# Wider weight splits, wider expert chunks and a convolution that reads its PSUM bank, in a two-layer diffusion trunk on one core

## Chip, cores and metric

One NeuronCore of a Trainium2 chip runs the whole program. The time is device microseconds of one execution, from launch to end. Its engines are TensorE (PE: matmuls; PEld: its weight loads), VectorE (DVE), ScalarE (ACT), GpSimd (POOL) and SyncE (SP, which here only issues DMAs and reads registers).

## The reference

Two layers work on 256 latent tokens (`x`) behind 256 context tokens (`ctx`), width 1024, all in fp32. Each layer is a token mixer and a channel mixer; the second layer's output is wanted for the latent tokens alone.

```python
for layer in range(2):
    u = h * (1 + mod[1]) + mod[0]                # mod: six vectors from c @ ada_w[layer]
    p = split_cols(u @ w_in[layer])              # 1024 -> 2048 columns
    lru  = rglru(centred_dwconv(p[0])) * gelu(p[1])      # conv of 4 taps, 256 channels
    swa  = windowed_attention(rope(p[2]), rope(p[3]), p[4], sink)   # 8 heads, 2 kv heads
    diff = diff_attention(rope(p[5]), rope(p[6]), p[7])  # 4 differential heads
    h = layer_norm(alpha * h + mod[2] * (concat([lru, swa, diff]) @ w_out[layer]))
    u = h * (1 + mod[4]) + mod[3]
    if layer == 0:
        f = (silu(u @ w1) * (u @ w3)) @ w2       # 1024 -> 2816 -> 1024, all 512 tokens
    else:                                        # 256 tokens, each to 2 of 8 experts
        f = sum(combine[:, e] * ((silu(u @ w1[e]) * (u @ w3[e])) @ w2[e]) for e in range(8))
    h = layer_norm(alpha * h + mod[5] * f)
```

`centred_dwconv` takes, for each channel, the taps at t-1, t, t+1 and t+2, over context and latent tokens apart, with zeros outside.

## The kernel before

**Precision and splits.** Matmuls run on fp32r operands. To keep fp32's accuracy each operand is split in two (`split`, L119, for weights; `split2`, L130, for activations): ScalarE casts it to `whi`, and VectorE subtracts `whi` from it into `wlo`. A product is three matmuls (`mm3`, L105): activation high with weight high, high with low, low with high. A weight tile of 1 MB (128 x 2048 fp32) comes by one DMA on SyncE's queue into `raw` (two buffers, L111) or, in the experts, `rawb` (seven buffers; `wtile`, L999, takes `rawb` and `raw` in turn, nine tiles in all). It is then split in two pieces of 128 x 1024 into the pool `wp` (L1254), which holds five pairs of `whi` and `wlo`. The dense down product has its own pool `wp2` of 1024. The SyncE queue issues loads in order; a load whose buffer is not yet free holds up those behind it.

**Order of the work.** The text of the program is not the order on the engines: the instructions of each engine are put in an order when the program is built, so that independent work interleaves. Each engine then runs its own list in order, and waits on semaphores.

**Layer by layer.** The conditioning products (`ada`, L243) are cut into steps that `fill` puts between other work. The mixer (L706) starts with `lru_products` (L401): the transposed products of the first 512 columns, four PSUM banks (two for the branch x that is convolved, from the tag `acc`, two for its gate, from `S`). `lru_in` (L436) copies an x bank to `xp`, padded, `lru_gate` (L445) makes the gelu, and the generator `lru` (L457) does the convolution (one `tensor_scalar`, three `scalar_tensor_tensor` on VectorE), its gates and its scans, in pieces that `fill_lru` hands out between the token blocks. Three chunks of 512 columns of `w_in` follow (`chunk`, L398; `half`, L390), then two streams of attention (`diff`, L643, and `swa`, L585), then the output projection (L767) and the norm. The dense feed-forward of layer 0 (`ffn`, L840) goes over 11 slices of 256 inner columns with weights stationary and 512 tokens moving.

**Experts.** `moe` (L1160) routes, then does seven units of work. A unit is one expert's block of up to 128 gathered tokens. The inner 2816 columns go in chunks (`CHUNKS`, L1009): five of 512 and one of 256. For a chunk, `up` (L1020) loads the tiles of w1 and w3 (`up_views`, L1011), splits them and multiplies into two of four PSUM banks `h`, then makes `g = silu(b1) * b3`; `turn_g` (L1045) transposes g and splits it; `down` (L1058) multiplies it with w2 into two banks `Y`. The loop (L1202 to L1222) puts the next chunk's `up` ahead of this chunk's `down`, with `turn_g` in the middle of `up`; the next unit's tokens are gathered at chunk `nch - 3` and turned at `nch - 2`. After a unit's last `down`, `scatter` (L1117) brings the rows back to their tokens: yh and yl, eight matmuls, four weightings `sct` on VectorE (two buffers) and four additions to `hl` on GpSimd. `moe_consts` (L1134) loads the router's constants on GpSimd's queue ahead of the second mixer.

Of the kernel before, what the change touches and what calls it, by code (L numbers as in the profile page):

```python
# [15 lines left out]
F32 = mybir.dt.float32  # L16
# [4 lines left out]
ALU = mybir.AluOpType  # L21
# [55 lines left out]
class Trunk:  # L77
# [41 lines left out]
    def split(self, v, pool=None):  # L119
# [3 lines left out]
        pool = pool or self.wp  # L123
        hi = pool.tile([P, 1024], F32R, name="whi", tag="whi")[:, 0:a * b].rearrange("p (a b) -> p a b", a=a)
        lo = pool.tile([P, 1024], F32R, name="wlo", tag="wlo")[:, 0:a * b].rearrange("p (a b) -> p a b", a=a)
# [310 lines left out]
    def lru_in(self, bx):  # L436

        nc = self.nc
        xp = self.lp.tile([P, 2, 260], F32, name="xp", tag="xp", bufs=2)
        nc.gpsimd.memset(xp[:, :, 0:1], 0.0)  # L440
        nc.gpsimd.memset(xp[:, :, 257:260], 0.0)
        nc.scalar.copy(out=xp[:, :, 1:257], in_=bx.rearrange("p (s t) -> p s t", s=2))
        return xp
# [13 lines left out]
    def lru(self, l, cb, xp, bd, y, t0):  # L457
# [3 lines left out]
        u = lp.tile([P, 2, 256], F32, name="u", tag="u")  # L461
        TS(u, xp[:, :, 0:256], self.convw(l, 0, cb), self.convb(l, cb), ALU.mult, ALU.add)
        for j in range(1, 4):
            STT(out=u, in0=xp[:, :, j:j + 256], scalar=self.convw(l, j, cb), in1=u, op0=ALU.mult, op1=ALU.add)
        u = u.rearrange("p s t -> p (s t)")
        yield
# [96 lines left out]
    def weights_t(self, p, nk):  # L563
# [5 lines left out]
        t = self.pp.tile([P, 512], F32, name="pT", tag="pT", bufs=4)  # L569
# [73 lines left out]
    def diff(self, l, tb, q, kT, V, mix, mp):  # L643
# [33 lines left out]
        m = mix  # L677
# [28 lines left out]
    def mixer(self, l, uh, ul, qtb, bd, products, prepare=None):  # L706
# [4 lines left out]
        t0 = 256 if lat else 0  # L711
        with tc.tile_pool(name="pp", bufs=4) as self.pp, tc.tile_pool(name="kv", bufs=1) as kp, tc.tile_pool(name="st", bufs=2) as self.sp, \
# [298 lines left out]
    def up_views(self, e, c0, n):  # L1011
# [3 lines left out]
        for name in ("moe_w1", "moe_w3"):  # L1015
            w = self.i[name][0, es].rearrange("o (k p) n -> p (o k) n", p=P)
            for k0 in range(0, KD, step):
                yield w[:, k0:k0 + step, c0:c0 + n]
# [373 lines left out]
```

## Time and profile before

| | |
|---|---|
| median of 3 runs | 1674.49 us (1672.95 to 1676.26) |
| profiled execution | 1673.18 us |
| its span, first to last instruction | 1671.3 us |
| mean granted TensorE clock | 0.975 |
| instructions | 21565 |
| moved by DMA | 364.77 MB, mean 218 GB/s |
| TensorE / VectorE / ScalarE / GpSimd busy | 95% / 73% / 55% / 10% of the span |

Lines L... are lines of the kernel before. A row of the profile names an instruction by its line, engine, operation and tiles (written <- read, buffer numbers left out); as helpers issue most of them, the tiles tell more than the line. A matmul's row lasts longer than its slot, since matmuls overlap in the array: its cost is the distance from one start to the next. "Idle before it <-X" is the time that the engine stood still before an instruction, and what released it; in a list of waits, "A <- B" is A waiting for B. [...] The stages of the span: conditioning and layer-0 mixer to about 315 us, dense feed-forward to 720, layer-1 mixer and projection to 915, routing to 942, experts to 1655, last norm and output to the end.

### The profile page before, as it was taken

Reading aid. Unit: us, or ns where it says so; the run is one execution under the profiler, and the core shown is the slowest. Engines: PE = TensorE matmul, PEld = TensorE weight load, DVE = VectorE, ACT = ScalarE, POOL = GpSimd, SP = SyncE. Lnnn points to the kernel's source line nnn. Section 1 sums busy time; section 2 is a strip of 40 time slices with the busy share of each in tenths; the row PEclk is TensorE's granted clock in tenths of the full one; section 3 lists DMA queues with packets and bytes.
Section 4 is the critical chain, followed back from the end, with each engine's and each line's share of the span. In section 5 each row is a group of like instructions: output and inputs, shape, how many; then the busy total and the mean of one; then the engine's idle time right before and its main releaser. Section 6 shows DMA issues by size and latency. Waiting matters only on the chain. (4 is left out here: it accounts for less than half of the span.)

```text
span 1671.3 us, 21565 instructions
## 1 busy us (share of the span) xinstructions
PE 1587.6 (95%) x7977; PEld 1229.7 (74%) x7977; DVE 1221.2 (73%) x1741; ACT 919.8 (55%) x1298; POOL 160.9 (10%) x131
## 2 busy tenths in 40 slices
PE   7999999999999999989899799999999999999995
PEld 3776566787777777777567588787887878878784
DVE  2678675644443345687976998989888898888987
ACT  2466565423222223246665487777776776767773
POOL 0000012250000000260002200101001010010101
PEclk8999999999999999989999799999999999999998
DMA  8313446224542354212348599898998989989890
GB/s 304 121 54 104 152 152 201 101 94 158 170 157 101 126 166 162 76 54 82 113 141 285 177 393 358 322 377 304 352 347 312 344 316 341 356 310 335 325 355 31
DMA packets 164582, 364.77 MB, mean 218 GB/s; under 512 B 8396, under 2 KB 46120, under 8 KB 159352
## 3 DMA queue, kind: packets, MB, share of 16 engines
q1 hardware_dynamic: 159472, 355.56, 60.6%
q0 software_dynamic: 1840, 6.67, 1.2%
q10 hardware_dynamic: 3160, 1.12, 0.3%
q8 instruction: 64, 1.05, 0.3%
q14 instruction: 46, 0.38, 0.1%
HBM read 362.27 MB, written 1.05 MB: 217 GB/s over the span
## 5 line engine op out<-in xcount | busy, mean ns | idle before, releaser
L127 DVE TENSOR_TENSOR wlo<-rawb,whi 128x1024 fp32r<-128x1024 f32 x362 | 436.0, 1249 | 34.5 <-ACT whi L126 30.6
L126 ACT CAST whi<-rawb 128x1024 fp32r<-128x1024 f32 x362 | 364.3, 1051 | 57.0 <-PE ps_h L109 33.6
L127 DVE TENSOR_TENSOR wlo<-raw,whi 128x1024 fp32r<-128x1024 f32 x214 | 269.2, 1279 | 100.1 <-ACT whi L126 98.7
L126 ACT CAST whi<-raw 128x1024 fp32r<-128x1024 f32 x214 | 218.7, 1051 | 183.8 <-DMA raw<-in_ffn_w_dram 85.6
L108 PE MATMUL ps_h<-wlo,th 128*128 128x512 f32 (+1 forms) x672 | 257.6, 383 | 14.2 <-DVE wlo L127 13.3
L107 PE MATMUL ps_h<-whi,th 128*128 128x512 f32 (+1 forms) x672 | 253.7, 378 | 0.2 <-ACT th L131 0.2
L109 PE MATMUL ps_h<-whi,tl 128*128 128x512 f32 (+1 forms) x672 | 251.8, 375 | 0.0
L108 PEld LDWEIGHTS ps_h<-wlo,th 128*128 128x128 f32 x672 | 127.3, 189 | 51.2 <-DVE wlo L127 30.6
L107 PEld LDWEIGHTS ps_h<-whi,th 128*128 128x128 f32 x672 | 127.5, 190 | 23.0 <-ACT th L131 0.5
L109 PEld LDWEIGHTS ps_h<-whi,tl 128*128 128x128 f32 x672 | 127.4, 190 | 20.6 <-DVE tl L132 0.2
L108 PE MATMUL ps_Y<-wlo,gTh 128*128 128x512 f32 x308 | 122.4, 397 | 0.4
L109 PE MATMUL ps_Y<-whi,gTl 128*128 128x512 f32 x308 | 120.2, 390 | 0.0
L1132 POOL TENSOR_TENSOR hl<-hl,sct 128x512 f32<-128x512 f32 x26 | 45.0, 1759 | 679.5 <-DVE sct L1131 559.5
L107 PE MATMUL ps_Y<-whi,gTh 128*128 128x512 f32 x308 | 108.4, 390 | 0.0
L107 PE MATMUL ps_acc<-uh,whi 128*128 128x512 f32 (+1 forms) x256 | 92.4, 367 | 2.6 <-ACT whi L126 2.3
L108 PE MATMUL ps_acc<-ul,whi 128*128 128x512 f32 (+1 forms) x256 | 94.1, 368 | 0.1
L109 PE MATMUL ps_acc<-uh,wlo 128*128 128x512 f32 (+1 forms) x256 | 92.1, 361 | 0.0
L108 PE MATMUL ps_S<-ul,whi 128*128 128x512 f32 (+1 forms) x240 | 85.7, 357 | 0.0
L107 PE MATMUL ps_S<-uh,whi 128*128 128x512 f32 (+1 forms) x240 | 85.6, 357 | 0.0
L109 PE MATMUL ps_S<-uh,wlo 128*128 128x512 f32 (+1 forms) x240 | 84.9, 355 | 0.0
L107 PE MATMUL ps_acc<-whi,uh 128*128 128x512 f32 (+1 forms) x176 | 71.0, 403 | 0.0
L108 PE MATMUL ps_acc<-wlo,uh 128*128 128x512 f32 (+1 forms) x176 | 69.1, 392 | 0.2 <-DVE wlo L127 0.2
(352 smaller groups left out, 2830.3 us busy)
## 6 DMA issues: line engine op xcount, KB each, us to landing
rawb<-in_moe_w_dram SPq DMA_DIRECT2D x181, 1024.0 KB, 6.7
raw<-in_moe_w_dram SPq DMA_DIRECT2D x50, 1024.0 KB, 6.5
raw<-in_ada_w_dram SPq DMA_DIRECT2D x40, 1024.0 KB, 4.9
raw<-in_ffn_w_dram SPq DMA_DIRECT2D x33, 1024.0 KB, 7.2
raw<-in_w_in_dram SPq DMA_DIRECT2D x16, 1024.0 KB, 5.6
aw<-in_ada_w_dram SPq DMA_DIRECT2D x16, 512.0 KB, 7.0
raw<-in_w_out_dram SPq DMA_DIRECT2D x16, 512.0 KB, 5.6
lg<-in_ln_g_dram POOLq DMA_DIRECT2D x4, 512.0 KB, 4.0
```

Of the source, the lines that this page charges most:

```text
L107: mm(out, lhsT=ah, rhs=bh, start=start, stop=False)
L108: mm(out, lhsT=ah, rhs=bl, start=False, stop=False)
L109: mm(out, lhsT=al, rhs=bh, start=False, stop=stop)
L126: nc.scalar.copy(out=hi, in_=v)
L127: self.last = nc.vector.tensor_tensor(out=lo, in0=v, in1=hi, op=ALU.subtract)
L1132: (nc.vector if quick and nn else nc.gpsimd).tensor_tensor(out=hl[:, b, cs], in0=hl[:, b, cs], in1=t, op=ALU.add)
```

## The change

- `split` works on up to 2048 columns at once; the pool `wp` has three pairs of 2048 where it had five of 1024. `wp2` keeps 1024. `half`, the projection and the dense `up` split a whole tile at a time.
- The experts' chunks are 1024, 1024 and 768 columns. Every tile of w1 and w3 is two row blocks of up to 1024 columns, so a DMA row is 4096 (or 3072) bytes where it was 2048 (or 1024). `up` fills two PSUM banks for w1 and two for w3, all four `h` banks; `turn_g` does two parts. The gather stands at chunk `nch - 2` and the turn at `nch - 1`, of three.
- `rawb` has six buffers where it had seven.
- `lru_in` is gone. `lru_conv` does the four operations of the convolution straight from the PSUM bank (the tap at t first, the others on the columns that they cover), for both blocks, ahead of the gates; the result `u` has two buffers. The x banks have the tag `S` and the gates' banks `acc`.
- `pT` has three buffers in layer 1 (four in layer 0); the four `mix` tiles become two rotating ones; `moe_consts` stands behind the second mixer.

```diff
-        pool = pool or self.wp
-        hi = pool.tile([P, 1024], F32R, name="whi", tag="whi")[:, 0:a * b]...
+        pool, n = (pool, 1024) if pool else (self.wp, 2048)
+        hi = pool.tile([P, n], F32R, name="whi", tag="whi")[:, 0:a * b]...
...
-        ws = []
-        for q in range(2):
-            wh, wl = self.split(r[:, 2 * q:2 * q + 2, :])
-            ws += [(wh[:, 0], wl[:, 0]), (wh[:, 1], wl[:, 1])]
-        return ws
+        wh, wl = self.split(r)
+        return [(wh[:, k], wl[:, k]) for k in range(4)]
...
-        bs = [self.bank("acc" if cb < 2 else "S") for cb in range(4)]
+        bs = [self.bank("S" if cb < 2 else "acc") for cb in range(4)]
...
+    def lru_conv(self, l, cb, bx):
+        nc = self.nc
+        x = bx.rearrange("p (s t) -> p s t", s=2)
+        u = self.lp.tile([P, 2, 256], F32, name="u", tag="u", bufs=2)
+        nc.vector.tensor_scalar(u, x, self.convw(l, 1, cb), self.convb(l, cb), ALU.mult, ALU.add)
+        for j, o, a, b in ((0, 1, 0, 255), (2, 0, 1, 256), (3, 0, 2, 256)):
+            v = u[:, :, o:o + b - a]
+            nc.vector.scalar_tensor_tensor(out=v, in0=x[:, :, a:b], scalar=self.convw(l, j, cb), in1=v, op0=ALU.mult, op1=ALU.add)
+        return u.rearrange("p s t -> p (s t)")
...
-            xs, bs = [], [*products][-1]
-            for cb in range(2):
-                xs.append(self.lru_in(bs[cb]))
+            bs = [*products][-1]
+            xs = [self.lru_conv(l, cb, bs[cb]) for cb in range(2)]
...
-                a, b = self.split(r[:, 0:4]), self.split(r[:, 4:8])
-                ws.append([(t[0][:, k], t[1][:, k]) for t in (a, b) for k in range(4)])
+                wh, wl = self.split(r)
+                ws.append([(wh[:, k], wl[:, k]) for k in range(KD)])
...
-    CHUNKS = [(c, min(512, FF - c)) for c in range(0, FF, 512)]
+    CHUNKS = [(c, min(1024, FF - c)) for c in range(0, FF, 1024)]
...
+        parts = [slice(p, min(p + 512, n)) for p in range(0, n, 512)]
...
+            bs = [self.bank("h")[:, 0:q.stop - q.start] for q in parts]
+            for t in range(4):
+                wh, wl = self.split(tiles[4 * j + t])
+                for kk in range(2):
+                    k = 2 * t + kk
+                    for b, q in zip(bs, parts):
+                        self.mm3(b, th[:, k], tl[:, k], wh[:, kk, q], wl[:, kk, q], k == 0, k == KD - 1)
+            hb.append(bs)
             if j == 0 and mid:
                 mid()
...
+        gs = []
+        for b1, b3, q in zip(*hb, parts):
+            g = self.mp.tile([P, 512], F32, name="g", tag="g")[:, 0:q.stop - q.start]
+            nc.scalar.activation(out=g, in_=b1, func=AF.Silu)
+            nc.vector.tensor_tensor(out=g, in0=g, in1=b3, op=ALU.mult)
+            gs.append(g)
...
-            r = self.wtile(w2[:, j0 + f0:j0 + f0 + 2, :])
-            for f in range(f0, f0 + 2):
-                wh, wl = self.split(r[:, f - f0:f - f0 + 1])
+            wh, wl = self.split(self.wtile(w2[:, j0 + f0:j0 + f0 + 2, :]))
+            for f in range(2):
...
-                if c == nch - 3 and u + 1 < UNITS:
+                if c == nch - 2 and u + 1 < UNITS:
                     x2, selT2 = self.gather(pu[:, :, u + 1], xh, xl)
-                if c == nch - 2 and u + 1 < UNITS:
+                if c == nch - 1 and u + 1 < UNITS:
                     x2 = self.turn(x2)
...
-            self.wp = pool("wp", 5)
+            self.wp = pool("wp", 3)
...
-            self.RB, self.wn = 7, 0
+            self.moe_consts(pool("rc", 1))
+            self.RB, self.wn = 6, 0
```

## Rows read from the trace of the kernel before

**Rows 1.** The page's first part: busy us, share of the span, instructions.

```profile
PE 1587.6 (95%) x7977; PEld 1229.7 (74%) x7977; DVE 1221.2 (73%) x1741; ACT 919.8 (55%) x1298; POOL 160.9 (10%) x131
```

**Rows 2.** Stretches: us, then busy PE, PEld, DVE, ACT, POOL; PEclk, DMA share, GB/s.

```profile
335.00:720.00 385.00, 378.55 (x1785) 297.71 (x1783) 185.34 (x234) 98.92 (x119) 40.54 (x24) 1.00 0.40 131
720.00:915.00 195.00, 182.54 (x1088) 137.23 (x1088) 151.81 (x308) 121.96 (x228) 30.14 (x29) 0.96 0.41 135
...
1052.90:1151.60 98.70, 98.02 (x468) 80.97 (x468) 91.25 (x89) 76.84 (x84) 7.01 (x4) 1.00 0.95 347
1151.60:1253.40 101.80, 100.02 (x470) 81.25 (x470) 90.14 (x89) 73.13 (x84) 7.03 (x5) 1.00 0.94 331
1253.40:1358.10 104.70, 101.64 (x469) 82.22 (x468) 91.07 (x90) 73.43 (x85) 7.02 (x5) 0.98 0.94 332
1358.10:1461.60 103.50, 100.39 (x469) 80.99 (x468) 90.97 (x90) 73.46 (x85) 7.02 (x5) 1.00 0.94 335
1461.60:1566.30 104.70, 101.66 (x469) 82.32 (x469) 90.76 (x88) 73.44 (x85) 7.01 (x5) 0.98 0.93 331
1566.30:1654.50 88.20, 85.06 (x396) 67.99 (x395) 76.74 (x74) 58.37 (x67) 7.02 (x5) 1.00 0.67 240
```

**Rows 3.** Timeline of GpSimd: start us, us, instructions merged; one scatter of six.

```profile
1253.39 7.02 POOL L1132 TENSOR_TENSOR hl<-hl,sct 128x512 f32<-128x512 f32 x4 [94.76 <-DVE sct L1131]
```

**Rows 4.** Waits of TensorE in the experts: us in total, times, longest us.

```profile
PE ps_h L108 <- DVE wlo L127: 13.3, 15, 1.2
```

**Rows 5.** Waits of the DMA queue on SyncE in the experts.

```profile
SPq L1006 <- DVE wlo L127: 521.3, 210, 7.5
```

**Rows 6.** Timeline of VectorE around the scatter at 1253 us.

```profile
1251.07 1.28 DVE L132 TENSOR_TENSOR yl<-ps_Y,yh 128x512 fp32r<-128x512 f32 x2
...
1253.91 1.87 DVE L127 TENSOR_TENSOR wlo<-rawb,whi 128x1024 fp32r<-128x1024 f32 x1
...
1256.96 0.75 DVE L1131 SCALAR_TENSOR_TENSOR sct<-ps_T,cu,gate 128x512 f32<-128x512 f32 x1 [0.51 <-POOL hl L1132]
1257.62 3.87 DVE L127 TENSOR_TENSOR wlo<-rawb,whi 128x1024 fp32r<-128x1024 f32 x2
...
1263.15 4.62 DVE L127 TENSOR_TENSOR wlo<-raw,whi 128x1024 fp32r<-128x1024 f32 x4
```

**Rows 7.** Timeline of ScalarE there.

```profile
1257.95 0.59 ACT L131 CAST gTh<-ps_T 128x512 fp32r<-128x512 f32 x1 [3.38 <-PE ps_T L1052]
...
1270.04 1.06 ACT L126 CAST whi<-rawb 128x1024 fp32r<-128x1024 f32 x1 [0.31 <-PE ps_Y L109]
```

**Rows 8.** ScalarE's groups in the experts: busy us, mean ns, idle before.

```profile
L126 ACT CAST whi<-rawb 128x1024 fp32r<-128x1024 f32 x357 | 359.1, 1051 | 50.3 <-PE ps_h L109 33.6 <-PE ps_Y L109 14.5 <-DVE wlo L127 1.5
...
L131 ACT CAST gTh<-ps_T 128x512 fp32r<-128x512 f32 x35 | 20.5, 585 | 43.8 <-PE ps_T L1052 43.8
```

**Rows 9.** VectorE's groups there.

```profile
L127 DVE TENSOR_TENSOR wlo<-rawb,whi 128x1024 fp32r<-128x1024 f32 x360 | 433.6, 1249 | 34.5 <-ACT whi L126 30.6
...
L1042 DVE TENSOR_TENSOR g<-g,ps_h 128x512 f32<-128x512 f32 x35 | 23.9, 683 | 12.6 <-PE ps_h L109 12.4
```

**Rows 10.** Timeline of TensorE, matmuls of 512: two rows six matmuls apart.

```profile
1101.05 0.39 PE L107 MATMUL ps_Y<-whi,gTh 128*128 128x512 f32 x1
...
1102.41 0.39 PE L107 MATMUL ps_Y<-whi,gTh 128*128 128x512 f32 x1
```

**Rows 11.** Instructions that touch xp: duration min/median/max, first and last start.

```profile
L464 DVE SCALAR_TENSOR_TENSOR u<-xp,col,u x12: 723/748/753, 67.8 to 798.6; 128x512 f32<-128x512 f32 x12
...
L442 ACT COPY xp<-ps_acc x4: 588/590/592, 66.6 to 748.5; 128x512 f32<-128x512 f32 x4
L462 DVE TENSOR_SCALAR u<-xp,col x4: 521/538/547, 67.3 to 793.9; 128x512 f32<-128x512 f32 x4
```

**Rows 12.** Waits of TensorE over the whole span.

```profile
PE ps_A L255 <- DMA raw<-in_ada_w_dram: 3.9, 2, 3.7
...
PE ps_acc L107 <- ACT whi L126: 2.7, 2, 2.3
```

More of the change, by code (lines that the diff above doesn't have):

```diff
@@ L455, in lru_gate, with lru @@
         nc.vector.scalar_tensor_tensor(out=xg, in0=gq, scalar=1.0, in1=xg, op0=ALU.add, op1=ALU.mult)
-    def lru(self, l, cb, xp, bd, y, t0):
+    def lru(self, l, cb, u, bd, y, t0):
         nc, lp = self.nc, self.lp
         TS, TT, STT, ACT = nc.vector.tensor_scalar, nc.vector.tensor_tensor, nc.vector.scalar_tensor_tensor, nc.scalar.activation
[L461 to L466, printed above, removed]
         hs = []
@@ L675, in diff @@
             yield "tail" if h0 + G == 8 else "head"
-        m = mix
+        m = self.rp.tile([P, 256], F32, name="mix", tag="mix", bufs=2)
         mv = m.rearrange("p (h d) -> p h d", h=4)
@@ L727, in mixer @@
             V = kp.tile([P, NTB, P], F32, name="V")
-            mix = {tb: kp.tile([P, 256], F32, name=f"mix{tb}") for tb in qtb}
             ws = self.chunk(view(1536))
@@ L1027, in up @@
         for j in range(2):
-            b = self.bank("h")
-            k = 0
-            for r in tiles[j * len(tiles) // 2:(j + 1) * len(tiles) // 2]:
-                half = 1024 // n
-                for h0 in range(0, r.shape[1], half):
-                    wh, wl = self.split(r[:, h0:h0 + half])
-                    for kk in range(half):
-                        self.mm3(b[:, 0:n], th[:, k], tl[:, k], wh[:, kk], wl[:, kk], k == 0, k == KD - 1)
-                        k += 1
-            hb.append(b)
+            bs = [self.bank("h")[:, 0:q.stop - q.start] for q in parts]
@@ L1042, in up @@
-        nc.vector.tensor_tensor(out=g[:, 0:n], in0=g[:, 0:n], in1=hb[1][:, 0:n], op=ALU.mult)
-        return g
-    def turn_g(self, c, g):
-        nc, mp = self.nc, self.mp
-        n = self.CHUNKS[c][1]
-        nf = n // P
-        pt = self.bank("T")
-        for f in range(nf):
-            nc.tensor.transpose(pt[:, f * P:(f + 1) * P], g[:, f * P:(f + 1) * P], self.eye)
-        gh = mp.tile([P, 4, P], F32R, name="gTh", tag="gTh")
-        gl = mp.tile([P, 4, P], F32R, name="gTl", tag="gTl")
-        self.split2(gh[:, 0:nf], gl[:, 0:nf], pt[:, 0:n].rearrange("p (f t) -> p f t", f=nf))
-        return gh, gl
+        gs = []
@@ new lines, in up, with turn_g @@
+        for b1, b3, q in zip(*hb, parts):
[3 more added lines that the diff above has]
+            gs.append(g)
+        return gs
+    def turn_g(self, c, gs):
+        nc, mp = self.nc, self.mp
+        out = []
+        for g in gs:
+            nf = g.shape[1] // P
+            pt = self.bank("T")
+            for f in range(nf):
+                nc.tensor.transpose(pt[:, f * P:(f + 1) * P], g[:, f * P:(f + 1) * P], self.eye)
+            gh = mp.tile([P, 4, P], F32R, name="gTh", tag="gTh")
+            gl = mp.tile([P, 4, P], F32R, name="gTl", tag="gTl")
+            self.split2(gh[:, 0:nf], gl[:, 0:nf], pt[:, 0:nf * P].rearrange("p (f t) -> p f t", f=nf))
+            out += [(gh[:, f], gl[:, f]) for f in range(nf)]
+        return out
```

33 lines of the change are left out of this document (12 added, 21 removed).

## The prediction

> **What bounds the kernel now.** Read the page's first part first: TensorE is busy 1587.6 us of the 1671.3 us span, VectorE 1221.2 us [rows 1]. So a shorter VectorE or ScalarE instruction is worth time only where TensorE waits for it. The table by stretch says where TensorE has holes [rows 2]. In the dense feed-forward (335 to 720 us) VectorE works 185 of 385 us and TensorE 379: nothing to win there. The layer-1 mixer and projection (720 to 915) leave TensorE idle 12.5 us at a mean clock of 0.96. Then come the experts; the windows are cut at the start of each unit's scatter, where GpSimd adds the result to hl [rows 3]. A unit lasts 98.7 us once, then 101.8, 104.7, 103.5 and 104.7 us; the last stretch (88.2 us, no following unit) holds 3.1 us of TensorE idle time. VectorE is busy 90 to 91 us in every full unit, so it is nearly as full as TensorE, and the long units are long because TensorE waits.
>
> The view of waits names whom for: inside the experts TensorE waits 15 times, 13.3 us, for wlo, the subtraction on VectorE, and for nothing else that counts [rows 4]. The DMA queue's own waits run the other way: SyncE waits 521 us, 210 times, for wlo, that is for a free landing buffer [rows 5]. Transfers are ahead of use; the splitting of weights is what is late.
>
> How late is seen at one unit's end [rows 3, 6, 7]. While GpSimd adds for 7.02 us, one subtraction takes 1.87 us and two take 3.87 us, against 4.62 us for four later. VectorE waits another 0.51 us for GpSimd to free a scatter buffer. ScalarE, whose queue is in order, stands 3.38 us before gTh because TensorE has not yet reached those transposes, and the casts queued behind gTh stand too. Then TensorE runs out of split weights.
>
> **The change, part by part.** Sums are made against the profiled execution (1673.18 us, span 1671.3); the median of the runs, 1674.49 us, is 0.1% above it.
>
> *Splits of 2048.* 554 of the 576 casts and as many subtractions become 277 of double width; the 22 splits of ffn's w2 keep their size. A cast of 1024 takes 1.051 us and one of 512 0.585 us [rows 8], so 512 more columns cost 0.466 us and a cast of 2048 about 1.98 us (estimate from these rows). A subtraction of 1024 back to back costs 4.62/4 = 1.155 us [rows 6]; an operation of 512 takes 0.683 us alone and one of 1024 in the mean 1.249 us [rows 9], with the slow ones at the scatter inside; I take 2.2 us back to back and 2.3 us alone for 2048. VectorE saves about 0.1 us a pair: 33 tiles a unit give 3.3 us of 90; over the kernel some 28 us of VectorE and 33 us of ScalarE (277 x 0.12). Outside the experts all of it lies beside TensorE.
>
> [...]
>
> *Buffers.* Five buffers of 1024 become three of 2048. In the steady state ScalarE starts a cast 0.3 us after TensorE frees a buffer [rows 7], and six matmuls of 512, which are the work of 1024 split columns, take 1.36 us [rows 10], 0.227 us each. Before: 0.3 + 1.05 + 1.2 = 2.6 us until the new half is ready, while four ready halves feed 5.44 us: margin 2.9 us. After: 0.3 + 2.0 + 2.3 = 4.6 us against two ready tiles, again 5.44 us: margin 0.85 us. So the change gives VectorE a faster recovery (2.2 us of work per 2.72 us instead of 2.31) and takes two thirds of the margin that covers a burst.
>
> *Chunks of 1024.* A unit has three turns (silu, g, transposes, gTh) instead of six, with two parts in each; the matmuls, transposes and bytes are the same. Fewer turns mean fewer places where ScalarE stands before gTh. All four h banks are filled by one chunk; the eight or six column blocks of the down product (at least 36 x 0.227 = 8.2 us) lie between that and the next fill, against 2 x 0.6 + 2 x 0.7 us to empty them: hidden. The turn after a scatter comes four tiles (10.9 us) behind it instead of half that, so the two bursts no longer meet.
>
> *The term.* Against the best unit, 98.7 us, the others lose 3.1, 6.0, 4.8 and 6.0 us, and the last stretch 3.1 us (its idle time): 23.0 us. Ends: all of it goes (-23), or rival D's +17. At a scatter I count VectorE's burst as yl 1.3 + four sct 3.0 + slowdown 2.3 us = 6.6 us [rows 6], less TensorE's own scatter 1.9 us, margin 0.85 us, recovery 4 x 0.5 us: about 1.8 us left of 3 to 6, and 0.3 us at each turn. That is some 60% of the 23: **-14 us**.
>
> *Longer runs, one landing buffer fewer (nine to eight).* With SyncE waiting for buffers all the time [rows 5], faster packets give nothing; the queue still runs 8 x 2.72 us ahead: 0. Without that cover one tile would cost 2.72 us a time.
>
> *Convolution from the bank.* Four copies xp (0.59 us each, ScalarE) and eight tiny memsets go. The four operations stay: before 0.54 + 3 x 0.75 = 2.8 us a block [rows 11]; from PSUM the first costs at most 0.75, so +0.2 us a block. No row shows this convolution on a bank; an operation of 512 with a PSUM operand (0.683 us) [rows 9] and the ones from SBUF (0.75) are the ends. Both blocks now stand before the gates, so 2.8 us of VectorE work comes ahead of the keys in each layer; behind it wait the gates, the next wlo and the keys' st, and for those the transposes. TensorE has the next token block (24 x 0.227 = 5.4 us) as cover. Bounds 0 to +2.9 a layer; I take +0.7 each: **+1.4 us**. Swapped banks: the gates' banks are copied out by ScalarE at once; 0.
>
> *First split.* TensorE waits 2.3 us for the very first cast now [rows 12]; the wider one adds 0.93 us and its subtraction 1.1 us. Bounds 0 (ada transfers pace that stretch) to +2: **+1.0**. The experts' first tiles: a 2.3 us subtraction between small routing steps, 0 to +1: **+0.5**.
>
> *Mixer weights.* Three whole tiles let the next chunk's first half be cast while the present two are in use, so its landing buffer is free sooner and ada loads follow sooner; one such load holds TensorE 3.7 us in layer 1 [rows 12]. Bounds -4 to +2 (it can also be pushed into another gap): **-1.5**. Router constants loaded after the mixer, three pT buffers, two mix buffers: first used behind the whole projection, or covered by the other attention stream; 0, at most +1.
>
> Sum: -14 + 1.4 + 1.0 + 0.5 - 1.5 = -12.6; 1673.2 - 12.6 = 1660.6, **forecast 1661 us**, own range 1653 to 1669.
>
> **Rivals.** (B) *All waiting for wlo goes*, since VectorE gains speed and meets fewer turns: -23, and the ada wait -4, the rest as above (+2.9): 1673.2 - 24.1 = 1649, its own range 1638 to 1653. For it: VectorE is at 87% in the long units. Against: the scatter burst itself stays.
>
> (C) *The gain is eaten at the scatter.* VectorE and GpSimd slow each other there [rows 3, 6]. If a subtraction once begun holds GpSimd off to its end, 1.1 us more of it delays each of the two adds for which the third and fourth sct wait: 2.2 us x 6 scatters = 13 us, and the time is 1673 to 1676. Against: in those 7.02 us VectorE did three subtractions and two sct, so neither shut the other out. [...]
>
> (D) *Slower: the third buffer is missed at the turns.* Place: the 21 turns, where ScalarE stands before gTh. A stand of 3.38 us [rows 7] less margin 0.85 and less the transposes' own 0.6 us leaves 1.9 us of TensorE waiting; 21 x 1.9 = 40 us, less the 23 won, +1.4 elsewhere: 1692. It decides from 23/21 = 1.1 us a turn. For it: the margin falls from 2.9 to 0.85. Against: the stand is short in most turns.
>
> **How the numbers follow.** Forecast 0.46, B 0.20, C 0.13, D 0.21. About 0.2% (3.3 us) is what a measurement of this kernel tells from no change. Faster: forecast and B, and a bit of C: 0.67; same: C, 0.13; slower: D, 0.20. The range 1640 to 1682 leaves out the low end of B and more than half of D.
>
> **What would show it.** Right: expert units of 98 to 101 us, TensorE's wait for wlo down from 13.3 us to 3 to 7, SyncE still waiting for wlo, VectorE about 87 us a unit, subtractions of 2.2 to 2.3 us. B: units at 97 to 98 us and no such wait. C: sct waiting over 1 us for GpSimd. D: a wait of whi or wlo at each of 21 turns. The forecast is wrong in its cause if the time moves outside 942 to 1655 us by over 4 us.

## The result, and the profile after

The changed kernel takes 1700.99 us (median of 4 runs, 1694.1 to 1702.17), the kernel before 1675.22 us beside it (4 runs): ratio 1.0147, 95% interval 1.0117 to 1.0177. It is 25.8 us slower where 13 us less were forecast. The profiled execution took 1700.04 us with a span of 1698.2 us and a mean granted clock of 0.969 (before 0.975). Its first part, to be read beside [rows 1]:

```profile
PE 1591.3 (94%) x7977; PEld 1234.2 (73%) x7977; DVE 1197.9 (71%) x1478; ACT 889.6 (52%) x1031; POOL 171.7 (10%) x123
```

VectorE and ScalarE did get cheaper, by 23 and 30 us. TensorE got no shorter, and its idle time grew from 83.7 to 106.9 us. The stretches answer to [rows 2]; from the third on each is an expert unit, cut at the start of its scatter (columns as there):

```profile
335.00:720.00 385.00, 379.79 (x1807) 300.31 (x1806) 176.77 (x207) 98.01 (x101) 33.40 (x19) 1.00 0.39 131
720.00:927.00 207.00, 190.62 (x1113) 141.74 (x1113) 155.56 (x313) 120.72 (x215) 34.05 (x32) 0.95 0.38 124
...
1081.60:1187.38 105.78, 101.40 (x470) 83.24 (x469) 89.37 (x59) 71.51 (x53) 9.15 (x5) 0.97 0.90 327
1187.38:1287.42 100.04, 97.92 (x466) 80.66 (x465) 87.15 (x58) 70.12 (x53) 9.14 (x4) 1.00 0.94 337
1287.42:1392.12 104.70, 99.66 (x469) 81.22 (x469) 89.45 (x59) 71.37 (x54) 9.16 (x4) 1.00 0.92 333
...
1496.77:1603.80 107.03, 102.00 (x479) 82.87 (x479) 91.10 (x57) 73.83 (x55) 9.16 (x4) 1.00 0.93 333
```

The matmuls of a unit are the same as before, but the boundary of these windows is not: each scatter now has 512 more columns of the next unit's `up` ahead of it. Whole experts are therefore compared from their first product to their last: 709.8 us before (941.7 to 1651.5), 725.1 after (952.9 to 1678.0). So 15.3 us were lost in the experts and 11.2 us ahead of them: 3.4 us by the end of layer 0's projection, 2.2 more until the feed-forward's first down product, 2.2 in the feed-forward and 3.4 in layer 1's mixer, projection and routing (each the shift of the same matmul between the two profiles).

In the experts, the waits of TensorE show four groups where [rows 4] had one that counted:

```profile
PE ps_h L108 <- DVE wlo L127: 16.0, 19, 1.2
PE ps_Y L108 <- DVE wlo L127: 6.8, 4, 1.7
PE ps_h L107 <- ACT th L131: 3.9, 2, 1.9
PE ps_h L109 <- DVE tl L132: 2.5, 2, 1.2
```

`th` and `tl` are the next unit's turned tokens. Where TensorE first waits for them (1042.8 us; once more at 1148.5), ScalarE and VectorE do this (start, us, instructions merged; in brackets the idle time before and who ended it):

```profile
1040.34 1.90 ACT L126 CAST whi<-rawb 128x2048 fp32r<-128x2048 f32 x1 [0.81 <-PE ps_Y L109]
1042.15 1.07 ACT L131 CAST th<-ps_T 128x512 fp32r<-128x512 f32 x2
```

```profile
1042.27 2.29 DVE L127 TENSOR_TENSOR wlo<-rawb,whi 128x2048 fp32r<-128x2048 f32 x1 [0.42 <-ACT whi L126]
1044.48 1.28 DVE L132 TENSOR_TENSOR tl<-ps_T,th 128x512 fp32r<-128x512 f32 x2
```

and TensorE this:

```profile
1040.14 0.71 PE L1106 MATMUL ps_T<-cst,xu 128*128 128x128 f32 x5
1042.78 0.50 PE L107 MATMUL ps_h<-whi,th 128*128 128x512 f32 x1 [1.93 <-ACT th L131]
...
1045.22 1.22 PE L109 MATMUL ps_h<-whi,tl 128*128 128x512 f32 x2 [1.25 <-DVE tl L132]
1046.24 0.63 PE L107 MATMUL ps_h<-whi,th 128*128 128x512 f32 x1
1046.67 0.63 PE L108 MATMUL ps_h<-wlo,th 128*128 128x512 f32 x1
```

The turn's last transpose ends at 1040.85 us. The `th` casts stand in ScalarE's queue behind a cast of 1.90 us, `tl` in VectorE's behind a subtraction of 2.29 us, and the next matmul needs both. TensorE stands 1.93 and 1.25 us. Its clock falls to half by the second wait: matmuls start 0.43 us apart (1046.24, 1046.67) where they start 0.227 us apart at full clock [rows 10]. The stretch behind the wait and the one after it, by the same columns as the stretches above:

```profile
1044.20:1050.90 6.70, 5.68 (x13) 4.46 (x14) 1.56 (x3) 1.86 (x1) 0.00 (x0) 0.50 0.89 361
1051.00:1057.00 6.00, 6.00 (x28) 4.97 (x27) 4.56 (x2) 3.47 (x2) 0.00 (x0) 1.00 0.43 138
```

The granted clock (PEclk) is 0.50 in the first of them and 1.00 in the second. Some eleven matmuls at 0.2 us more are 2.2 us on top of the 3.2 us of waiting, and the second such turn, at 1148.5 us, goes the same way (1.93 and 1.25 us of waiting again, then matmuls 0.43 us apart). At three of the four later turns (1346.2, 1450.9 and 1555.6 us) TensorE stands 1.73 us before a `ps_Y<-wlo` instead, for the weights queue up behind `th` and `tl` in turn; at the turn of 1250 us it does not stand. The fourth wait of this group, at 1659.5 us, is in the last unit, which has no turn behind it.

### The profile page after: what moved, and what is told of

Its sections match the earlier page's. It is cut to its first block, busy times and chain, and to the rows that moved or that the text cites. A ratio compares the mean times of both kernels' runs of the same rounds, so it can differ in the third digit from the quotient of the medians.

```text
span 1698.2 us, 20910 instructions
## 1 busy us (share of the span) xinstructions
PE 1591.3 (94%) x7977; PEld 1234.2 (73%) x7977; DVE 1197.9 (71%) x1478; ACT 889.6 (52%) x1031; POOL 171.7 (10%) x123
## 5 line engine op out<-in xcount | busy, mean ns | idle before, releaser
L127 DVE TENSOR_TENSOR wlo<-rawb,whi 128x2048 fp32r<-128x2048 f32 (+1 forms) x185 | 405.6, 2213 | 55.2 <-ACT whi L126 54.0
L126 ACT CAST whi<-rawb 128x2048 fp32r<-128x2048 f32 (+1 forms) x185 | 334.6, 1812 | 113.7 <-PE ps_h L109 71.2
L127 DVE TENSOR_TENSOR wlo<-raw,whi 128x2048 fp32r<-128x2048 f32 (+2 forms) x128 | 268.7, 2107 | 109.2 <-ACT whi L126 108.5
L126 ACT CAST whi<-raw 128x2048 fp32r<-128x2048 f32 (+2 forms) x128 | 219.5, 1717 | 204.8 <-DMA raw<-in_ffn_w_dram 64.0
L107 PE MATMUL ps_h<-whi,th 128*128 128x512 f32 (+1 forms) x672 | 243.7, 378 | 4.5 <-ACT th L131 4.5
L1126 POOL TENSOR_TENSOR hl<-hl,sct 128x512 f32<-128x512 f32 x26 | 57.8, 2252 | 682.6 <-DVE sct L1125 544.2
L107 PE MATMUL ps_S<-uh,whi 128*128 128x512 f32 (+1 forms) x256 | 91.5, 359 | 0.4 <-ACT whi L126 0.4
L109 PE MATMUL ps_S<-uh,wlo 128*128 128x512 f32 (+1 forms) x256 | 91.0, 356 | 0.0
L108 PE MATMUL ps_acc<-ul,whi 128*128 128x512 f32 (+1 forms) x240 | 86.6, 361 | 2.5 <-DVE ul L132 2.5
L108 PEld LDWEIGHTS ps_Y<-wlo,gTh 128*128 128x128 f32 x308 | 57.8, 188 | 21.4 <-DVE wlo L127 9.2
```

The source lines that it names most:

```text
L107: mm(out, lhsT=ah, rhs=bh, start=start, stop=False)
L108: mm(out, lhsT=ah, rhs=bl, start=False, stop=False)
L109: mm(out, lhsT=al, rhs=bh, start=False, stop=stop)
L126: nc.scalar.copy(out=hi, in_=v)
L127: self.last = nc.vector.tensor_tensor(out=lo, in0=v, in1=hi, op=ALU.subtract)
L1126: (nc.vector if quick and nn else nc.gpsimd).tensor_tensor(out=hl[:, b, cs], in0=hl[:, b, cs], in1=t, op=ALU.add)
```

## The experiments

Each was timed in five rounds beside the kernel before, whose median in the five groups of runs was 1673.41, 1671.6, 1672.29, 1671.4 and 1671.36 us; the ratios are to that. "Experts" is again first product to last product in one profiled execution; among versions with the same turn and splits there it lies within 1.5 us (703.8 to 705.3). What lies ahead of the experts scatters more: the first expert product came at 943.0 us in one version below and at 948.1 in another whose code ahead of it is the same.

### The turn's place

**Turn a chunk ahead**, in the changed kernel:

```diff
-                if c == nch - 2 and u + 1 < UNITS:
+                if c == nch - 3 and u + 1 < UNITS:
                     x2, selT2 = self.gather(pu[:, :, u + 1], xh, xl)
-                if c == nch - 1 and u + 1 < UNITS:
+                if c == nch - 2 and u + 1 < UNITS:
                     x2 = self.turn(x2)
```

> The changed kernel with one thing moved: the next unit's tokens are gathered at chunk nch-3 and turned at nch-2, a whole chunk of 1024 ahead of their use, as far ahead (in chunks) as in the kernel before. Theory 1 (the turn now stands directly ahead of the product that reads it: 6.4 us at two units, about 2 us at four): 17 to 22 us less than the changed kernel, 1679 to 1684 us; TensorE no longer waits for th and tl behind the turn (2.1 and 1.4 us each now), and the half-clock stretches there are gone. Rival (the loss in the experts is the third buffer missed at scatters and turns, as rival D of the prediction had it): at most 3 us less, 1697 to 1702 us, with TensorE's wait for wlo still 16 us or more.

1680.97 us, ratio 1.0041 (1.0020 to 1.0061). Experts 705.1 us, 20.0 us less than in the changed kernel. The waits there:

```profile
PE ps_h L108 <- DVE wlo L127: 13.3, 18, 1.2
PE ps_Y L108 <- DVE wlo L127: 1.7, 1, 1.7
PE ps_h L107 <- ACT th L131: 0.7, 1, 0.7
```

`tl` is gone, `th` holds TensorE 0.7 us once (at the very first product), and the stretch at the same time runs at full clock with more than twice the matmuls (31 for 13):

```profile
1044.20:1050.90 6.70, 6.70 (x31) 5.57 (x30) 5.84 (x3) 4.94 (x3) 0.00 (x0) 1.00 1.01 405
```

So the turn's place costs some 18 us (1.0147 less 1.0041 of 1673) to 20 us: the largest part of the loss, and the first theory. Most of the 20.0 us can be counted in the changed kernel: 5.4 us at each of the first two turns (two waits and the lower clock), 1.73 us at three later ones and 2.7 us more before `ps_h<-wlo`, together 18.6 us.

**Turn late, in the kernel before**: gather at `nch - 2`, turn at `nch - 1` of six chunks, nothing else (the reverse of the edit above).

> The kernel before with one thing moved: gather at nch-2 and turn at nch-1 of its six chunks, so that the turn stands directly ahead of the product that reads it, as in the changed kernel. Theory 1 (that place costs by itself, whatever the chunk): 10 to 20 us more than before, 1682 to 1692 us, with waits for th and tl of 2.1 and 1.4 us behind the first turns. Rival (it costs only where one chunk fills all four h banks): within 3 us of before.

1673.38 us, ratio 1.0011 (1.0002 to 1.0019): the expectation of 10 to 20 us missed, the rival holds. TensorE waits for `th` 1.5 us in two waits, and the mean granted clock of the profiled execution, 0.977, is no lower than before (0.975). At the first of them ScalarE does this, and the turn's last transpose ends at 1035.85 us:

```profile
1035.01 1.05 ACT L126 CAST whi<-raw 128x1024 fp32r<-128x1024 f32 x1 [0.32 <-PE ps_Y L109]
1035.97 1.06 ACT L131 CAST th<-ps_T 128x512 fp32r<-128x512 f32 x2
```

`th` starts 0.12 us behind the transposes here and 1.30 us behind them in the changed kernel. The place is cheap in the kernel before, where what queues ahead of `th` is short, and costs 18 us together with long instructions and long chunks. Which of those two makes it dear was not separated.

**Chunks of 512 in the changed kernel**, whole tiles still split at once (and the turn at `nch - 2` of six):

```diff
-    CHUNKS = [(c, min(1024, FF - c)) for c in range(0, FF, 1024)]
+    CHUNKS = [(c, min(512, FF - c)) for c in range(0, FF, 512)]
...
+            for r in tiles[j * len(tiles) // 2:(j + 1) * len(tiles) // 2]:
+                wh, wl = self.split(r)
+                for kk in range(r.shape[1]):
+                    self.mm3(b[:, 0:n], th[:, k], tl[:, k], wh[:, kk], wl[:, kk], k == 0, k == KD - 1)
+                    k += 1
```

> The changed kernel with the experts' chunks of 512 again (gather at nch-3, turn at nch-2 of six; up, turn_g and the DMA rows as before), the splits still 2048 wide in three buffers. Theory 1 (in the experts the turn's place is the loss, and wide splits cost nothing): 15 to 25 us less than the changed kernel, 1676 to 1686 us, units of 99 to 103 us. Rival D (three buffers missed at the turns): no gain or a loss, since the turns are six a unit again: 1699 to 1715 us, with more wlo waits than the 16 us of the changed kernel.

1681.91 us, ratio 1.0047 (1.0034 to 1.0060); experts 705.1 us. The same as with chunks of 1024 and the turn ahead. TensorE waits for `wlo` 11.1 us before `ps_h` and 1.3 us before `ps_Y`, though the turns of g are six a unit again: rival D is out.

**Chunks of 1024 alone**, in the kernel before, with splits of 1024 in five buffers:

```diff
+            for t in range(4):
+                for kk in range(2):
+                    wh, wl = self.split(tiles[4 * j + t][:, kk:kk + 1])
```

> The kernel before with the experts' chunks of 1024 alone (longer DMA rows, all four h banks a chunk, turn at nch-2 of three, so a chunk ahead); splits stay 1024 wide in five buffers, seven landing buffers in rawb. Theory 1 (chunk size is worth nothing by itself, the gain in the experts is the wide split's): within 3 us of before, 1671 to 1677 us. Rival (the gain comes from fewer turns and longer DMA rows): 4 to 8 us less than before, 1666 to 1670 us.

1673.22 us, ratio 1.0010 (1.0002 to 1.0019), experts 709.6 us: chunks and longer DMA rows gain nothing by themselves, as the prediction had it.

### Ahead of the experts

**Old convolution in the changed kernel** (`lru_in`, `xp` and the bank tags of before):

```diff
...
-            xs = [self.lru_conv(l, cb, bs[cb]) for cb in range(2)]
...
+            for cb in range(2):
+                xs.append(self.lru_in(bs[cb]))
```

> The changed kernel with the convolution of before: x banks from acc and gates from S, copied to xp, and the four operations inside the generator. Theory 1 (the bank tags and the convolution ahead of the gates disturb the two mixers, and make most of the 11 us lost ahead of the experts): 6 to 10 us less than the changed kernel, 1691 to 1695 us. Rival (those 11 us come from splits of 2048, which stand as single long pieces ahead of activations on ScalarE and VectorE): within 3 us of the changed kernel, 1698 to 1704 us.

1697.98 us, ratio 1.0141 (1.0119 to 1.0162) against 1.0147: at most 1 to 3 us back. Theory 1 falls; the rival's range holds, and what its cause is worth is measured below (5 us).

**The convolution's part alone in the kernel before**, the same edit the other way:

> The kernel before with the convolution's part of the change alone (four operations on the bank, ahead of the gates; x banks S, gates' banks acc). Theory 1 (bank tags and place make most of the loss ahead of the experts): 6 to 10 us more than before, 1681 to 1685 us, TensorE slow between the last product of layer 1's x banks and its first scan. Rival (the prediction's own term): +1.4 us, 1674 to 1678 us.

1682.4 us, ratio 1.0059 (1.0043 to 1.0074): 9 us by the medians, as theory 1 had it, and not the 1.4 predicted.

**The four operations ahead of the gates, still from `xp`**, bank tags as before:

```diff
...
+            xs = [self.lru_conv(l, cb, xs[cb]) for cb in range(2)]
             for cb in range(2):
                 self.lru_gate(cb, bs[2 + cb], t0, y)
```

> The kernel before with one thing moved: the four operations of the convolution stand ahead of the gates for both blocks, still from the copies xp, with the bank tags of before. Theory 1 (of the 9 us that the convolution's part costs alone, the place is the larger share, 2.8 us being the tags): 4 to 8 us more than before, 1676 to 1680 us. Rival (it is the reading from the bank, which keeps the x banks until the four operations are done): within 2 us of before.

1678.88 us, ratio 1.0041 (1.0026 to 1.0057). **The bank tags alone**:

```diff
-        bs = [self.bank("acc" if cb < 2 else "S") for cb in range(4)]
+        bs = [self.bank("S" if cb < 2 else "acc") for cb in range(4)]
```

> The kernel before with the bank tags alone exchanged (x banks S, gates' banks acc), still with xp and the convolution in its generator. Theory 1 (the tags make the loss of the convolution's part, since keys, transposes and conditioning then ask for the banks in another order): 6 to 10 us more than before, 1680 to 1684 us. Rival (it is the four operations ahead of the gates): within 2 us of before, 1672 to 1676 us.

1674.39 us, ratio 1.0016 (1.0007 to 1.0025). Place 6.6 us and tags 2.8 us make the 9, which leaves nothing for reading from the bank. What the place does stands in layer 1 of the kernel with the early operations: VectorE's order, and TensorE's waits from 738 us to the router.

```profile
751.32 0.53 DVE L448 TENSOR_SCALAR u<-xp,col 128x512 f32<-128x512 f32 x1
751.88 1.54 DVE L450 SCALAR_TENSOR_TENSOR u<-xp,col,u 128x512 f32<-128x512 f32 x2
...
757.32 1.22 DVE L127 TENSOR_TENSOR wlo<-raw,whi 128x1024 fp32r<-128x1024 f32 x1
```

```profile
PE ps_acc L108 <- DVE wlo L127: 2.4, 2, 2.2
PE ps_A L255 <- DMA raw<-in_ada_w_dram: 2.0, 1, 2.0
PE ps_S L658 <- ACT p L663: 1.8, 1, 1.8
PE ps_T L570 <- DVE nb L659: 1.6, 1, 1.6
PE ps_acc L675 <- ACT pT L574: 1.5, 1, 1.5
```

All eight operations of the two blocks stand ahead of the keys' `wlo`, where the kernel before has four, and TensorE waits 2.2 us for it. Three more waits of 1.5 to 1.8 us appear in the attention behind, where the kernel before has none over 0.7 us: moving VectorE work re-orders the streams that follow. From 720 us to the router this profile lost 6.2 us against before; 2.2 for the keys and some 3 to 4 in the attention, less 1.7 won at the conditioning load, make most of it. That the attention's waits come from the moved work is inferred from their absence before.

**Turn ahead and old convolution, splits of 2048 everywhere:**

> The changed kernel with the turn a chunk ahead and the convolution of before, splits 2048 wide everywhere. It is the link between two runs: if the parts add up, 1677 to 1679 us, 3 us less than with the turn alone put back and 6 us more than with 1024-wide pieces outside the experts. Rival (the two kernels' difference was the convolution's): 1671 to 1674 us, and long pieces outside the experts cost nothing.

1676.56 us, ratio 1.0030 (1.0016 to 1.0043). **The same with pieces of 1024 outside the experts**, in the same three buffers of 2048 (`cuts` gives the whole tile in the experts and pieces of 1024 outside):

```diff
+        for q in self.cuts(a, b):
+            nc.scalar.copy(out=hi[:, q], in_=v[:, q])
+            self.last = nc.vector.tensor_tensor(out=lo[:, q], in0=v[:, q], in1=hi[:, q], op=ALU.subtract)
```

> The changed kernel with the turn a chunk ahead, the convolution of before, and outside the experts every split written as casts and subtractions of 1024 columns into the same three buffers of 2048. Theory 1 (the 10 us lost ahead of the experts come from long single instructions in front of short ones on ScalarE and VectorE, so 1024-wide pieces give them back): 1667 to 1671 us, below the kernel before by the 5 us that the experts win. Rival (they come from the buffers: a buffer of 2048 is free only as a whole): 1676 to 1681 us, as the same kernel with long pieces would take.

1672.1 us (12 runs, 1667.44 to 1674.3), ratio 1.0000 (0.9991 to 1.0009); experts 703.8 us. Long pieces outside the experts cost the 5 us between these two, which have the same buffers, so the rival of the second is out, though its time lies a little above theory 1's range. One place in the changed kernel: ScalarE at the entry of the feed-forward (timeline), and what TensorE waits for that activation over the span (view of waits):

```profile
318.30 3.68 ACT L126 CAST whi<-raw 128x2048 fp32r<-128x2048 f32 x2
321.88 1.01 ACT L378 ACTIVATE u<-ps_S,adac,adac 128x256 f32<-128x256 f32 x2
```

```profile
PE ps_S L375 <- ACT u L378: 7.3, 7, 3.4
```

Two whole casts stand ahead of the activation. Before, the wait is 4.9 us with a longest of 1.6. The version ties with the kernel before although its experts are 6 us shorter, so by the medians something is still lost ahead of them. How much is not settled: its own profiled execution, 1668.23 us, was one of the shorter and shows 1.4 us, and three later versions with this code ahead of the experts show 3.0, 6.5 and 6.4.

### What a wide split is worth, and what the waits are made of

**Pieces of 1024 everywhere**, three buffers of 2048:

> As the kernel with 1024-wide pieces outside the experts, but with these pieces inside the experts too, so that three buffers of 2048 and chunks of 1024 stay and the long instructions are gone everywhere. Theory 1 (the experts gain from the fixed time saved on every pair of instructions): 4 to 8 us more than that kernel, VectorE busy about 3 us more a unit. Rival (the experts gain from six half buffers where there were five): the same within 2 us.

1679.79 us, ratio 1.0045 (1.0033 to 1.0057): inside the experts the long instructions are worth 7.5 us, as theory 1 said, though VectorE is busy 1.7 us more a unit and not 3. Pieces of 1024 in a buffer of 2048 come free only together; against chunks of 1024 with five buffers of 1024 (709.6 us above) the experts with long splits, 703.8 us, are 5.8 us shorter.

**Four pairs of 2048 in the experts, four landing buffers in `rawb`; five pairs and two; three pairs and four** (the edit of the first; the second has 2 in `wx`, the third has none):

```diff
+        self.wx = pool("wx", 1, "right")
...
+            pool = self.wx if self.sn % 4 >= 3 else self.wp
```

> The kernel with the turn a chunk ahead, the convolution of before and 1024-wide pieces outside the experts (the version that ties with before), with a fourth pair of 2048 for the experts' splits, and four landing buffers in rawb where there were six. Theory 1 (what TensorE still waits for wlo, 12.9 us in 17 waits, is the short margin of three buffers at scatters and turns): a fourth adds 2.7 us of margin, most of the waits go, 7 to 11 us less: 1661 to 1665 us. Rival (the waits are set by the order of VectorE's and ScalarE's work, or two landing buffers fewer cost as much): within 3 us, 1669 to 1675 us.

> The same with five pairs of 2048 for the experts' splits and two landing buffers in rawb (four with raw). Theory 1: no more than 3 us less than with four pairs, since the waits are nearly gone; 1659 to 1665 us if four landing buffers are enough. Rival (transfers then come late, TensorE waiting for rawb or whi behind a DMA): more than the version with four, 1670 us or above.

> The version that ties with before (turn a chunk ahead, old convolution, 1024-wide pieces outside the experts) with four landing buffers in rawb where it has six, and still three pairs. Theory 1 (the two landing buffers cost what the version with a fourth pair lost): 1675 to 1679 us. Rival (a fourth pair moves ScalarE's and VectorE's order for the worse, landing buffers cost nothing): 1671 to 1674 us.

1677.33 us (1.0029, 1.0017 to 1.0040), 1691.1 us (1.0099, 1.0083 to 1.0115) and 1672.08 us (1.0007, 0.9998 to 1.0016). The first theory of each missed. Two landing buffers fewer cost nothing; a fourth pair gains nothing and is even 4 us slower, for which no cause was found; the loss with five pairs and two landing buffers was not taken apart either. But the waits decide the question. TensorE in the experts with three pairs (first fence) and with four (second):

```profile
PE ps_h L108 <- DVE wlo L128: 12.9, 17, 1.2
PE ps_Y L108 <- DVE wlo L128: 1.7, 1, 1.7
```

```profile
PE ps_h L108 <- DVE wlo L131: 14.1, 17, 1.2
PE ps_Y L108 <- DVE wlo L131: 1.7, 1, 1.7
```

As many, as long, with one pair more: the wait is not for a free buffer. Before one of them (TensorE stands 0.95 us at 1245.6), ScalarE of the version with three pairs:

```profile
1237.37 1.91 ACT L127 CAST whi<-rawb 128x2048 fp32r<-128x2048 f32 x1 [0.81 <-PE ps_h L109]
1242.13 0.60 ACT L1047 ACTIVATE g<-ps_h 128x512 f32<-128x512 f32 x1 [2.85 <-PE ps_h L109]
1242.62 1.90 ACT L127 CAST whi<-rawb 128x2048 fp32r<-128x2048 f32 x1
```

It stands 2.85 us before a silu whose bank TensorE is still filling, and the next cast stands behind it.

**The silu queued behind the next cast** (`finish` makes g = silu(b1) * b3 of the chunk that `up` has just multiplied):

```diff
+            wh, wl = self.split(self.wtile(w2[:, j0 + f0:j0 + f0 + 2, :]))
+            if f0 == 0 and finish:
+                with self.tc.issue_after(self.cast.ins):
+                    gs = finish()
```

> The version that ties with before, with the two silu of a chunk queued on ScalarE behind the cast of the next tile (the first of w2) where they stood ahead of it. Theory 1 (what is left of TensorE's wait for wlo is the order on ScalarE: it stands 2.9 us before a silu whose bank TensorE is still filling, and the casts stand behind it; a fourth buffer left these waits where they were): the 0.95 us wait ahead of each scatter goes, 4 to 6 us less, 1666 to 1668 us. Rival (the wait only moves one tile on): within 2 us, 1670 to 1674 us.

1664.04 us, ratio 0.9949 (0.9933 to 0.9965), experts 694.4 us: theory 1, with more gain than it said. ScalarE no longer stands before the silu (timeline), and TensorE's waits in the experts are halved (view of waits):

```profile
1252.04 1.92 ACT L127 CAST whi<-raw 128x2048 fp32r<-128x2048 f32 x1 [0.81 <-PE ps_h L109]
1253.86 1.07 ACT L1048 ACTIVATE g<-ps_h 128x512 f32<-128x512 f32 x2
1254.82 1.92 ACT L127 CAST whi<-raw 128x2048 fp32r<-128x2048 f32 x1
```

```profile
PE ps_h L108 <- DVE wlo L128: 7.1, 10, 1.2
```

**The scatter's `yh` behind the next cast too:**

```diff
+                pre = self.split(self.wtile(next(views))), views
+                late.enter_context(tc.issue_after(self.cast.ins))
+            with late:
+                self.scatter(Y, selT, cu[:, :, u], gate, hl, u == UNITS - 1)
```

> The same with the scatter's yh casts queued behind the first cast of the following tile too. Theory 1 (order on ScalarE): the 1.2 us wait behind each scatter goes as well, 1660 to 1664 us, units of 99 us. Rival (that wait is VectorE's burst beside GpSimd's additions, which an order on ScalarE leaves alone): the same as with the silu alone, within 2 us.

1661.06 us, ratio 0.9936 (0.9924 to 0.9948). The interval overlaps that of the silu alone and the waits are the same (6.9 us in 9): no gain is shown, so the rival holds. It is the fastest version of all, 0.6% below the kernel before and 2.1% below the changed one.

**Buffers outside the experts as fine as the pieces** (six buffers of 2048; outside, one holds `whi` and `wlo` of 1024 columns):

```diff
+        elif self.wide:
+            hi, lo = self.wp.tile([P, 2048], F32R, name="whi", tag="w"), self.wp.tile([P, 2048], F32R, name="wlo", tag="w")
+        else:
+            t = self.wp.tile([P, 2048], F32R, name="w", tag="w")
+            hi, lo = t[:, 0:1024], t[:, 1024:2048]
```

> The version with silu and scatter behind the next cast, with the buffers outside the experts as fine as the pieces: six buffers of 2048 in one pool, each holding whi and wlo of 1024 columns outside the experts (six pairs that come free one by one), and a whole whi or wlo of 2048 inside them (three pairs). Theory 1 (what is still lost ahead of the experts, some 2 to 6 us, is that a buffer of 2048 comes free only as a whole): 1655 to 1659 us, the experts' first product no later than in the kernel before. Rival (that loss is the smaller pT and mix buffers or where the router's constants load): as without it, 1660 to 1664 us.

1663.33 us, ratio 0.9955 (0.9941 to 0.9968): no gain, theory 1 falls. What is still lost ahead of the experts stays open; the smaller `pT`, `mix` and the place of the router's constants, which the versions share with the changed kernel, were not tested.

**The silu behind the next two casts in the kernel before:**

> The kernel before with each chunk's silu queued on ScalarE behind the two casts of the first tile of w2 that follow it. Theory 1 (the order on ScalarE and the wide split each give their own part: there the waits for wlo stand at the scatter, behind VectorE's burst, and four ready halves cover a stand of 2.9 us): within 4 us of before, 1667 to 1673 us. Rival (the order alone gives the whole gain, and wide splits are not needed): 1661 to 1665 us.

1678.25 us, ratio 1.0039 (1.0026 to 1.0052): slower, against both expectations. There the waits for `wlo` grow from 13.3 us in 15 to 14.4 us in 18, the longest from 1.2 to 1.9 us. So the order alone does not give the gain, and not every move of a standing instruction is one. Whether it takes the wide splits or the chunks of 1024 as well was not separated.

## Why the prediction was wrong

By the ratios, in steps from the version that ties with before: long pieces outside the experts +5.0 us, the convolution on top of them +1.9, the turn's place on top of both +17.7: 24.6 us together, the whole of the loss. The 1.9 is within the noise of its two runs. The tie itself is a gain of 6 to 7.5 us for long instructions in the experts against as much lost elsewhere, which no run found. The time moved by 11.2 us outside the experts, which the prediction itself had named as a sign that its cause is wrong, and the waits for `wlo` rose from 13.3 to 22.8 us where 3 to 7 were forecast.

**The failed step.** "Chunks of 1024 ... the matmuls, transposes and bytes are the same" was priced at nothing but the turns of g. The diff also moves the token turn from `nch - 2` to `nch - 1`, and for the moved step nothing was counted: that `th` and `tl` are read by the very next product, and that a 1.9 us cast and a 2.3 us subtraction can stand ahead of them. That is 18 to 20 us of the 25.8. No row of before showed this wait [rows 4], but the prediction's own sizes were enough to bound it: a cast of 2.0 us and a subtraction of 2.3 us at each of six turns. Only the direction of rival D came true: it forecast a slower kernel, 1692 us, for another reason.

**Splits of 2048.** Sizes right: the cast takes 1.91 us (1.98 said), the subtraction 2.29 alone (2.3) and 4.49 for two back to back (2.2 each); VectorE won 23 us of the 28 said, ScalarE 30 of 33. The count was off: 554 pieces of 1024 become 235 of 2048 and 56 of 1536, not 277, since tiles of the last chunk, 768 wide, have 1536 columns. The saving was smaller too: subtractions of 1024 that follow each other directly start 1.136 us apart, those of 2048 2.202 us, so a pair saves 0.07 us and not 0.1. In the experts the wide split is worth 6 to 7.5 us, about half the term of 14. "Outside the experts all of it lies beside TensorE" was wrong: 5 us lost where whole casts stand ahead of activations.

**Buffers and the term.** The margin was the wrong model. A fourth pair left the waits at 17; the order on ScalarE makes half of them. [rows 7] showed a stand of this kind: ScalarE stood 3.38 us before gTh there. The prediction read that row as a burst to be covered and not as an order to be changed. The stand that counted with wide splits was the one before the silu, though, and moving the silu in the kernel before gained nothing. With turn and silu mended the experts take 15.4 us less than before (694.4 against 709.8). That this is about the size forecast is luck: 9.4 us of it came with the silu's new place, an order that the prediction did not consider.

**Rival C and the scatter.** Against C the prediction held that "neither shut the other out". The rows after read otherwise. VectorE and GpSimd at one scatter:

```profile
1287.95 2.92 DVE L127 TENSOR_TENSOR wlo<-rawb,whi 128x2048 fp32r<-128x2048 f32 x1
1290.80 0.74 DVE L1125 SCALAR_TENSOR_TENSOR sct<-ps_T,cu,gate 128x512 f32<-128x512 f32 x1
1292.06 0.75 DVE L1125 SCALAR_TENSOR_TENSOR sct<-ps_T,cu,gate 128x512 f32<-128x512 f32 x1 [0.52 <-POOL hl L1126]
```

```profile
1287.42 1.30 POOL L1126 TENSOR_TENSOR hl<-hl,sct 128x512 f32<-128x512 f32 x1 [90.90 <-DVE sct L1125]
1288.69 3.34 POOL L1126 TENSOR_TENSOR hl<-hl,sct 128x512 f32<-128x512 f32 x1
```

The first addition ends at 1288.72; the subtraction begun at 1287.95 ends at 1290.87, 0.77 us beside that addition and 2.15 behind it, where one that stands alone takes 2.29. The second addition, until 1292.03, ends 1.16 us after the subtraction, where the first took 1.30 in all. So each row's length is about the other's rest plus its own work, also in [rows 6]: 1.87 us from 1253.91, 0.78 of it beside the addition that ends at 1254.69. Read so, a subtraction and an addition took turns here, which is inferred from these lengths; no run tests it. The sct at 1290.80, which reads PSUM, takes 0.74 us beside the same addition (all 24 take 0.74 to 0.75): it does not stand. That is what the prediction's "neither shut the other out" missed: rows that overlap can still take turns, with the standing inside the row. So the four additions take 9.15 us where they took 7.02 [rows 3], the 2.1 us that C had. Yet C's price did not come: the sct wait for GpSimd is 0.52 us as before, since that sct stands behind the same subtraction on VectorE anyway.

**Convolution.** Said +1.4, measured 9 us alone. The operations themselves cost nearly what was said (from the bank 0.80 us for the first, at most 0.75 said, and 0.74 for the others); the keys' `wlo` behind them was named but its cover overrated, and the re-ordered attention was not thought of. In the changed kernel it is worth less (1.0041 against 1.0030 without it, intervals that overlap): parts that disturb the same stretch need not add.

**Right.** Landing buffers at 0; chunk size and longer DMA rows at 0 by themselves; rival D out (the waits for `wlo` stand at scatters and behind one silu a unit, not at each of 21 turns of g); the router's load and the first split too small to see. The conditioning load in layer 1 holds TensorE 2.3 us in two waits where it was 3.7 in one.

## What to carry to other kernels

When a diff changes how many pieces a loop has, look at every step that hangs on a piece's number: the same "one ahead of the end" can move a step from a chunk before its use to directly in front of it. On these engines, which run their lists in order, a longer instruction was cheaper in sum (2.20 us from the start of one subtraction of 2048 columns to the next, against 2.27 for two of 1024) and dearer to whatever stood behind it: it gained 6 to 7.5 us where nearly all work is of its kind and lost 5 us where small steps feed TensorE. When TensorE waits for a split, look at what stands ahead of it on ScalarE before adding buffers, and measure a changed order in the kernel that is to have it.

## What the runs showed of the hardware

Two waits of 1.93 and 1.25 us within 4.4 us went with 6.7 us at a granted clock of 0.50, from within the second wait on, which cost another 2.2 us. Shorter waits left the clock at 1.00 at some places and not at others: in the kernel before, TensorE stands 0.83, 1.16 and 0.82 us behind the scatter at 1253 us and then runs at half clock, and behind the scatter at 1358 us with 0.84, 1.16 and 0.79 us it does not (the 0.98 and 1.00 of [rows 2]). The half clock behind the first of these two (columns of [rows 2]):

```profile
1261.80:1265.00 3.20, 3.20 (x8) 2.46 (x8) 3.20 (x4) 1.51 (x2) 0.00 (x0) 0.50 0.79 247
```

A subtraction of 1024 columns beside GpSimd's additions of 128x1024 in layer 1 takes far longer than at a scatter: 3.4 us, where four that follow each other take 4.62 us [rows 6]. VectorE (first two lines) and GpSimd in the kernel before:

```profile
743.96 3.42 DVE L127 TENSOR_TENSOR wlo<-raw,whi 128x1024 fp32r<-128x1024 f32 x1
747.30 3.43 DVE L127 TENSOR_TENSOR wlo<-raw,whi 128x1024 fp32r<-128x1024 f32 x1
...
743.45 2.84 POOL L837 TENSOR_TENSOR hl<-hl,lb 128x1024 f32<-128x1024 f32 x1
746.26 3.39 POOL L837 TENSOR_TENSOR hl<-hl,lb 128x1024 f32<-128x1024 f32 x1
```

That fits turns as well: each subtraction ends 1.1 us after an addition does (746.29 and 749.65 us), and the 2.3 us of its row before that are then standing. The first question at such a long VectorE row is what GpSimd does beside it.
